# The low part of the keys in zero-filled tiles: a second scores pass over all 128 rows

## The chip, the cores and the metric

The kernel runs on one core of one Trainium2 chip. The metric is the time of one execution in device microseconds (us), taken as the median of several runs. One run was also recorded by the hardware profiler; its rows give start and length of each instruction on TensorE (PE, and PEld for its weight loads), VectorE (DVE), ScalarE (ACT) and GpSimd (POOL).

## The reference

Two blocks of two layers each work on 512 positions of width 1024. The parts that the change touches are the scores of three attentions:

```
# block 1: per head h of 6, head dim 64, three dilations mixed; per query row
scores = q_h @ k_h.T * 64**-0.5 - slope_h * distance          (masked)
# block 2, indexer: 8 heads of dim 64, one shared key
I[t, s] = sum_h w[t, h] * relu(q_idx[t, h] . k_idx[s])         (top 256 kept)
# block 2, sparse attention: 8 heads of dim 64
logits = q_h @ k_h.T * 64**-0.5                                (only the kept keys)
```

Around them lie dense projections (input, output, feed-forward), a depthwise convolution, a gated recurrence in each layer and normalisations. Inputs and outputs are float32.

## The kernel before

Activations are held channel-major: a tile is 128 channels (partitions) by 512 positions. TensorE takes float32 operands in a rounded form, so the kernel splits an operand into a high part H (the rounded value, cast on ScalarE) and a low part L (the remainder, a subtraction). A dense product is three matmuls per 128 channels, `mm3` at L332 to L334: H times H, L times H, H times L. Weights are loaded as `wraw`, split into `wH` (L311, ScalarE) and `wL` (L312, GpSimd), and used.

A head has 64 channels, so two heads (even and odd) share a 128-row tile, in rows 0 to 63 and 64 to 127. For the scores of one head, `q_part` builds a tile `qs` with the high part of its queries in the head's own 64 rows and the low part in the other 64 (L834, L835), and `qk_parts` builds `ks` with the high part of the keys in both halves (L845, L846). The first matmul of the scores (L894) takes all 128 rows: high queries times high keys plus low queries times high keys. The second (L895) adds high queries times low keys: it takes the 64 rows `r` of the head alone, since the low keys `kl` (L847) fill only those rows. The indexer does the same at L1291 and L1292, with low keys `kL` written into both halves once per layer (L1266).

The low keys are tiles of a rotating pool. In block 1 they share the tag `rS` with `qs`, `ks` and with the operands of the recurrence (L737, copied at L738), six buffers in all, one low tile for the two heads of a pair; in block 2 they have a tag `kl` of two buffers. `ltag` names it.

The order of the work comes from Python generators that are woven together with fixed costs: in block 1 the recurrence and then six heads of dilated attention (`heads(0)` for even and `heads(1)` for odd heads, the second two steps behind), the dense products that fill TensorE in between, and the convolution; in block 2 the indexer's eight heads beside dense products, and later eight heads of sparse attention beside dense products. After a head's scores come the softmax (`softmax_rows`: L856 on VectorE, L451 on ScalarE, L858 and L859 on VectorE), a transpose on TensorE (L867), a split of the weights (L311, L312) and the product with the values (L625, L626). Each engine executes its instructions in a fixed order, which the framework lays out when the kernel is built.

Of the kernel before, what the change touches and what calls it, by code (L numbers as in the profile page):

```python
# [9 lines left out]
F32 = mybir.dt.float32  # L10
F32R = mybir.dt.float32r
# [7 lines left out]
S = 512  # L19
# [228 lines left out]
class Net:  # L248
    def __init__(self, tc, I, out, es):
        self.tc, self.nc, self.I, self.out = tc, tc.nc, I, out  # L250
        self.n = 0
        self.other = self.pinned = self.unpin = None
        self.ntmp, self.vbufs, self.nv = 4, 2, 3
        self.qtag = self.ktag = self.ltag = ("rS", 6)
        self.pending = []
        self.gate = None
        nc = self.nc
        pool = lambda name, **k: es.enter_context(tc.tile_pool(name=name, bufs=1, **k))
        self.cp = pool("const")
        self.wp = pool("wts")  # L260
        self.hp = pool("hid")
        self.ps = pool("psum", space=PSUM)
        self.xd = es.enter_context(tc.tile_pool(name="xd", bufs=1, space=bass.MemoryType.DRAM))
        self.ident = self.one(self.cp, [128, 128], "ident")
        self.bones = self.one(self.cp, [128, 128], "bones")
        self.ones = self.one(self.cp, [128, 128], "ones")
        nc.vector.memset(self.ones, 1.0)
# [374 lines left out]
class Recurrence:  # L642
# [88 lines left out]
    def operands(self, n, Q, K):  # L731

        N, m = self.N, S // (2 * n)
        view = lambda t, d: pattern(t, 0, (d, 2), (2 * n, m), (1, n))
        out = []
        for t in (K, Q):
            x = N.tile(self.P, [128, S], "rS", 6)  # L737
            N.nc.scalar.copy(view(x, n), view(t, S + n))  # L738
            out.append(x)
        return out  # L740
# [95 lines left out]
    return qs, r  # L836


def qk_parts(N, P, q, k, kl, odd, scale):

    nc = N.nc
    qs, r = q_part(N, P, q, odd, scale)
    o = slice(0, 64) if odd else slice(64, 128)
    ks = N.tile(P, [128, S], *N.ktag, F32R)
    N.behind(nc.scalar.copy(ks[r], k[r]))  # L845
    N.behind(nc.scalar.copy(ks[o], k[r]))  # L846
    nc.vector.tensor_sub(kl[r], k[r], ks[r].bitcast(F32))  # L847
    return qs, ks, kl, r


def softmax_rows(N, P, p, bias, w):
# [17 lines left out]
    N.split(SH[:, :nk, o], SL[:, :nk, o], p[:, :nk])  # L869


def key_parts(N, P):
    return N.tile(P, [128, S], *N.ltag, F32R)


def attention_head(N, P, q, k, kl, vt, h, out, bias, e, causal):


    nc = N.nc
    v = head_values(N, P, vt, h)  # L880
    qh, kh, klo, r = qk_parts(N, P, q, k, kl, e == 1, 0.125)
    yield 1
    for a in range(2):
        W = weight_tiles(N, P)
        nk = 2 + 2 * a if causal else 4
        if causal:
            for y in W:
                nc.gpsimd.memset(y[:, nk - 1, :128].bitcast(F32), 0.0)
        for t in (2 * a, 2 * a + 1):
            tk = slice(128 * t, 128 * t + 128)  # L890
            n = t + 1 if causal else 4
            w, wm = 128 * n, max(256, 128 * n)
            p = N.bank("s")
            nc.tensor.matmul(p[:, :wm], qh[:, tk], kh[:, :wm], start=True, stop=False)  # L894
            nc.tensor.matmul(p[:, :wm], qh[r, tk], klo[r, :wm], start=False, stop=True)  # L895
            s = softmax_rows(N, P, p, bias(t), w)
            yield 1
            transpose_probs(N, s, n, t, *W)
            if t % 2:
                yield 1  # L900
                weighted_values(N, P, v, *W, out[:, 256 * a:256 * a + 256], nk)
        yield 1


def dilated_head(N, P, h, q, k, kl, vt, out):
    tab = N.tile(P, [128, 896], "rW", 2)
    N.nc.sync.dma_start(tab, N.I["alibi"][h])
    return attention_head(N, P, q, k, kl, vt, h + 6, out, lambda t: tab[:, 384 - 128 * t:896 - 128 * t], h % 2, False)


def opening(N, P, c, mod, vec):
# [34 lines left out]
def block1_layer(N, l, mod, vec, sib, src, step, hs, ready):  # L946
    nc, I = N.nc, N.I
    N.drop_x()
    with N.tc.tile_pool(name="mix1", bufs=1, reuse_waits="tile") as P:
# [3 lines left out]
            take(p)  # L953

        rec = Recurrence(N, P, vec, l, sib)
        vt, pads, qk = {}, [], {}
        orec = [N.tile(P, [128, S], "orec", 3) for _ in range(3)]
        oatt = [N.tile(P, [128, S], "oatt", 3) for _ in range(3)]
# [33 lines left out]
                yield from cm(base + j, take)  # L992
            qk[j] = ts

        sg, ys, kls, done = [], [None, None], {}, set()
        mixed, first = [], {}
        order = (5, 6, 7, 0, 1, 2, 3, 4)
        chain = itertools.chain
# [1 line left out]
        def heads(e):  # L1000
            if e == 0:
                for j in range(3):
                    yield from rec.pair(j, vt, orec[j])
                N.lnexp()
                done.add("rec")
            yield from ready_when(lambda: "rec" in done, 1)
            for j in range(3):
                yield from ready_when(lambda: j in qk and (2 * j + e + 6) // 4 in vt, 1)
                if j not in kls:
                    kls[j] = key_parts(N, P)  # L1010
                yield from dilated_head(N, P, 2 * j + e, *qk[j], kls[j], vt, oatt[j][64 * e:64 * e + 64])
                done.add((j, e))

        def conv():
# [228 lines left out]
def index_parts(N, P, p, rope):  # L1243

    nc = N.nc
    mc = N.tile(P, [128, S], "tmp", N.ntmp)
    nc.scalar.copy(mc, p)
    glr = N.tile(P, [96, 2, S], "W", 6, F32R)
    one = N.tile(P, [32, S], "tmp", N.ntmp)
    nc.gpsimd.memset(one, 1.0)  # L1250
    nc.vector.tensor_copy(one[:16], mc[96:112])
    stacked(N, glr[:, 0], one, (1, 0))
    p = N.bank("t", [128, 4, 32])
    for t in range(4):
        nc.tensor.transpose(p[:, t], mc[64:96, 128 * t:128 * t + 128], N.ident[64:96, 64:96])
    w8 = N.tile(P, [128, 4, 8], "w8", 1)
    nc.vector.tensor_scalar(w8, p[:, :, :8], 8.0 ** -0.5, None, op0=OP.mult)
    end = rope.begin(mc)
    kH = N.tile(P, [128, S], *N.ktag, F32R)
    kL = N.tile(P, [128, S], *N.ltag, F32R)  # L1260

    def keys():
        end()
        for r in (slice(0, 64), slice(64, 128)):
            nc.scalar.copy(kH[r], mc[:64])
            nc.vector.tensor_sub(kL[r], mc[:64], kH[:64].bitcast(F32))  # L1266
    return glr, w8, kH, kL, keys


def stacked(N, out, src, low):  # L1270
# [7 lines left out]
            nc.scalar.copy(o, src)  # L1278


def index_scores(N, P, iq, w8, kH, kL, sc):

    nc = N.nc
    for h in range(8):
        yield from ready_when(lambda: len(iq) > h // 2, 1)
        qs, r = q_part(N, P, iq[h // 2], h % 2, 0.125)
        for t in range(1, 4):
            w = 128 * (t + 1)
            tk = slice(128 * t, 128 * t + 128)
            p = N.bank("s")  # L1290
            nc.tensor.matmul(p[:, :w], qs[:, tk], kH[:, :w], start=True, stop=False)  # L1291
            nc.tensor.matmul(p[:, :w], qs[r, tk], kL[r, :w], start=False, stop=True)  # L1292
            y = N.tile(P, [128, S], "tmp", N.ntmp)
            nc.scalar.activation(y[:, :w], p[:, :w], AF.Relu)
            if h == 0:
                nc.vector.tensor_scalar(sc[t][:, :w], y[:, :w], w8[:, t, 0:1], None, op0=OP.mult)
            else:
                nc.vector.scalar_tensor_tensor(sc[t][:, :w], y[:, :w], w8[:, t, h:h + 1], sc[t][:, :w],
                                               op0=OP.mult, op1=OP.add)
            yield 1  # L1300
    for t in range(1, 4):
        w = 128 * (t + 1)
        nc.vector.memset(sc[t][:64, w - 64:w], -1e30)
# [16 lines left out]
def sparse_attention(N, P, aq, ak, vt, bias, outs):  # L1320
    def heads(e):
        for j in range(4):
            if j not in kl:
                kl[j] = key_parts(N, P)
                out[j] = N.tile(P, [128, S], "tmp", N.ntmp)
            yield from attention_head(N, P, aq[j], ak[j], kl[j], vt, 2 * j + e, out[j][64 * e:64 * e + 64],
                                      lambda t: bias[t][:, :128 * t + 128], e, True)
            done.add((j, e))
            if {(j, 0), (j, 1)} <= done:
                outs[j] = (N.tile(P, [128, S], "X", 8, F32R), N.tile(P, [128, S], "X", 8, F32R))  # L1330
                N.split(*outs[j], out[j], N.nc.gpsimd)

    kl, out, done = {}, {}, set()
    return heads(0), delay(heads(1), 5, 1)


# [208 lines left out]
def block2(N, hs, ready, out):  # L1545
    nc, I = N.nc, N.I
    N.ntmp, N.vbufs, N.nv = 4, 2, 4
    N.qtag, N.ktag, N.ltag = ("qs", 2), ("ks", 2), ("kl", 2)
    with N.tc.tile_pool(name="b2", bufs=1) as B:
        tri = N.one(B, [128, 128], "tri", F32R)  # L1550
        with N.tc.tile_pool(name="tri", bufs=1) as P:
# [12 lines left out]
        for l in range(2):  # L1564
# [5 lines left out]
            with N.tc.tile_pool(name="mix2", bufs=1, reuse_waits="tile") as P:  # L1570
# [4 lines left out]
                N.gate = None  # L1575
                sc = [b0] + [N.tile(P, [128, S], "sc", 3) for _ in range(3)]
                rope = Rope(N, P, tab)
                glr, *keys, parts = index_parts(N, P, ready[0], rope)
                N.soon(8, parts)
                gla = Gla(N, P, l, tri, chunks, vec)  # L1580
# [85 lines left out]
```

## Time and profile before

| | |
|---|---|
| median of 3 runs | 3408.36 us (3407.62 to 3408.36) |
| the profiled execution's own time | 3403.52 us |
| its span, first to last instruction | 3401.7 us |
| PE, DVE, POOL, ACT busy | 96%, 52%, 51%, 47% of the span |
| mean granted TensorE clock | 0.983 |

The busy time of TensorE is not to be read as TensorE at its peak: its rows are pipelined, so that two of them overlap, and their ends are modelled. What tells how long a matmul holds TensorE is the distance from its start to the start of the next one.

### The profile page before, as it was taken

To read this page: it belongs to the slowest core of one execution; us is meant where nothing else is said; L and a number is where in the kernel's file an instruction comes from. 1 tells how busy PE (TensorE), PEld (TensorE's weight loads), DVE (VectorE), ACT (ScalarE), POOL (GpSimd) and SP (SyncE) were. 2 spreads that over 40 slices of the span, in tenths; PEclk is the share of its full clock that TensorE was granted. 3 is DMA by queue.
4 is the path that set the end of the run, shared out by engine and by line. 5 is a ranking of instruction groups with operands and counts; after the bars stand their busy time and mean duration, and the time that the engine had idled before them with its cause. 6 is when DMAs were issued, how large, how long until landed. Compare 5 with 4: busy or idle time off the path is not lost.

```text
span 3401.7 us, 46240 instructions
## 1 busy us (share of the span) xinstructions
PE 3263.0 (96%) x16546; PEld 2655.2 (78%) x16546; DVE 1777.1 (52%) x3029; ACT 1589.6 (47%) x3104; POOL 1744.5 (51%) x1442
## 2 busy tenths in 40 slices
PE   8799999998899999999999999999999999999998
PEld 6677787787766888887878777888878787778887
DVE  8987677607976633226740735332367407353332
ACT  4457543334466544435343645443353436454433
POOL 5542366555542455553445447565634454476654
PEclk9899999999899999999999999999999999999999
DMA  6323355542212322332213132333322131322232
GB/s 231 108 71 99 115 176 178 179 132 97 87 46 68 103 99 96 99 108 86 87 57 101 52 108 81 98 97 93 102 76 87 57 101 51 108 81 98 96 94 80
DMA packets 174445, 338.92 MB, mean 100 GB/s; under 512 B 20388, under 2 KB 27428, under 8 KB 174215
## 3 DMA queue, kind: packets, MB, share of 16 engines
q1 hardware_dynamic: 174214, 335.97, 31.1%
q8 instruction: 130, 2.13, 0.3%
q14 instruction: 101, 0.82, 0.1%
HBM read 325.28 MB, written 8.91 MB: 98 GB/s over the span
## 4 chain that ended last, share of the span: by engine, by line
PE 76%; DVE 11%; issue 4%; ACT 3%; POOL 3%; DMA 2%; SPq 0%; POOLq 0%; ACTq 0%; DVEq 0%
PE p L332 22%; PE p L333 21%; PE p L334 21%; POOL wL L312 2%; DVE cv L566 2%; PE s L706 2%; DVE ada L528 1%; DMA ada<-in_w_ada 1%; PE s L1424 1%; PE s L895 1%; PE t L867 1%; PE o L625 1%; PE o L626 1%; PE s L894 1%; DVE rW L746 1%
## 5 line engine op out<-in xcount | busy, mean ns | idle before, releaser
L312 POOL TENSOR_TENSOR wL<-wraw,wH 128x512 fp32r<-128x512 f32 x996 | 1334.6, 1348 | 1278.4 <-ACT wH L311 1184.3
L332 PE MATMUL p<-hH,wH 128*128 128x512 f32 (+1 forms) x2808 | 1080.9, 386 | 12.2 <-ACT hH L311 7.5
L333 PE MATMUL p<-hL,wH 128*128 128x512 f32 (+1 forms) x2808 | 1069.5, 381 | 12.7 <-POOL hL L312 10.2
L334 PE MATMUL p<-hH,wL 128*128 128x512 f32 (+1 forms) x2808 | 1065.5, 380 | 6.2 <-POOL wL L312 6.2
L311 ACT CAST wH<-wraw 128x512 fp32r<-128x512 f32 x996 | 607.0, 613 | 947.9 <-PE p L333 436.9
L332 PEld LDWEIGHTS p<-hH,wH 128*128 128x128 f32 x2808 | 536.4, 191 | 122.4 <-issue 14.0
L333 PEld LDWEIGHTS p<-hL,wH 128*128 128x128 f32 x2808 | 537.4, 191 | 111.1 <-POOL hL L312 12.2
L334 PEld LDWEIGHTS p<-hH,wL 128*128 128x128 f32 x2808 | 536.8, 191 | 107.2 <-POOL wL L312 10.0
L1142 DVE SCALAR_TENSOR_TENSOR y<-p,vec,y 128x511 f32<-128x511 f32 (+1 forms) x264 | 196.8, 748 | 484.9 <-ACT y L1139 297.4
L332 PE MATMUL p<-aH,wH 128*128 128x512 f32 (+1 forms) x704 | 266.5, 379 | 2.9 <-ACT aH L311 2.9
L333 PE MATMUL p<-aL,wH 128*128 128x512 f32 (+1 forms) x704 | 266.5, 379 | 0.6 <-POOL aL L312 0.6
L334 PE MATMUL p<-aH,wL 128*128 128x512 f32 (+1 forms) x704 | 265.6, 377 | 0.6 <-POOL wL L312 0.6
L332 PE MATMUL p<-wH,hH 128*128 128x256 f32 x704 | 202.4, 287 | 0.0
L333 PE MATMUL p<-wL,hH 128*128 128x256 f32 x704 | 201.4, 286 | 0.0
L334 PE MATMUL p<-wH,hL 128*128 128x256 f32 x704 | 200.3, 284 | 0.0
L528 DVE SCALAR_TENSOR_TENSOR ada<-ada,c 128x1024 f32<-128x1024 f32 x96 | 144.2, 1502 | 44.3 <-DMA ada<-in_w_ada 43.6
L312 POOL TENSOR_TENSOR aL<-y,aH 128x512 fp32r<-128x512 f32 x88 | 113.9, 1295 | 98.2 <-ACT aH L311 98.2
L332 PEld LDWEIGHTS p<-aH,wH 128*128 128x128 f32 x704 | 133.2, 189 | 27.7 <-ACT aH L311 3.4
L333 PEld LDWEIGHTS p<-aL,wH 128*128 128x128 f32 x704 | 133.1, 189 | 25.8 <-POOL aL L312 1.1
L334 PEld LDWEIGHTS p<-aH,wL 128*128 128x128 f32 x704 | 133.1, 189 | 25.5 <-POOL wL L312 1.0
L706 PE MATMUL s<-rS,rS 64*128 64x128 f32 (+1 forms) x864 | 111.6, 317 | 33.9 <-DVE rW L761 21.2
L332 PEld LDWEIGHTS p<-wH,hH 128*128 128x128 f32 x704 | 135.8, 193 | 3.7 <-issue 2.9
(338 smaller groups left out, 4736.9 us busy)
## 6 DMA issues: line engine op xcount, KB each, us to landing
ada<-in_w_ada SPq DMA_DIRECT2D x96, 512.0 KB
wraw<-in_w1up SPq DMA_DIRECT2D x176, 256.0 KB
wraw<-in_w2up SPq DMA_DIRECT2D x176, 256.0 KB
wraw<-in_w2cm SPq DMA_DIRECT2D x164, 256.0 KB
wraw<-in_w1dn SPq DMA_DIRECT2D x80, 256.0 KB
wraw<-in_w2dn SPq DMA_DIRECT2D x80, 256.0 KB
wraw<-in_w1cm SPq DMA_DIRECT2D x72, 256.0 KB
wraw<-in_w2tm SPq DMA_DIRECT2D x64, 256.0 KB
```

The source lines that it names most:

```text
L311: self.nc.scalar.copy(H, src)
L312: (eng or self.nc.vector).tensor_sub(L, src, H.bitcast(F32))
L332: self.product = first = mm(out, a[0], b[0], start=start, stop=False, **kw)
L333: mm(out, a[0], b[1], start=False, stop=False, **kw)
L334: mm(out, a[1], b[0], start=False, stop=stop, **kw)
L528: ins = nc.vector.scalar_tensor_tensor(w, w, 1.0, c, op0=OP.mult, op1=OP.mult, accum_out=mod[:, j:j + 1])
L566: nc.vector.scalar_tensor_tensor(y, pad[:, j:j + S], w, y, op0=OP.mult, op1=OP.add)
L625: nc.tensor.matmul(o, v[:, i], SH[:, i], start=i == 0, stop=False)
L626: nc.tensor.matmul(o, v[:, i], SL[:, i], start=False, stop=i == n - 1)
L706: N.nc.tensor.matmul(p[:, at:at + w], K[r, ks], Q[r, qs], start=True, stop=True)
L746: nc.vector.tensor_mul(view(Q), view(Q), pattern(t, 1, (b - 1, 2), (2, m), (0, n)))
L1142: nc.vector.scalar_tensor_tensor(y[:, -d:], p[:, :S + d], c[:, i:i + 1], y[:, -d:], op0=OP.mult, op1=OP.add)
```

## The change

Two tiles `kz0` and `kz1` per layer replace the rotating low-key tiles. `low_keys` makes them at the start of a layer's mixing stage and fills with zeros, on GpSimd, the half that the heads of the other parity use: rows 64 to 127 of `kz0`, rows 0 to 63 of `kz1`. Even heads write their low keys into rows 0 to 63 of `kz0`, odd heads into rows 64 to 127 of `kz1`, so the other half stays zero. The second matmul of the scores then takes all 128 rows of `qs` and of `kz`; the low queries meet zeros. The tag `rS` gets five buffers in place of six, the tag `kl` goes away. Nothing else is edited.

```diff
-        self.qtag = self.ktag = self.ltag = ("rS", 6)
+        self.qtag = self.ktag = ("rS", 5)
...
-            x = N.tile(self.P, [128, S], "rS", 6)
+            x = N.tile(self.P, [128, S], "rS", 5)
...
+def low_keys(N, P):
+    N.kz = [N.one(P, [128, S], f"kz{e}", F32R) for e in range(2)]
+    for e, t in enumerate(N.kz):
+        N.nc.gpsimd.memset(t[64 - 64 * e:128 - 64 * e].bitcast(F32), 0.0)
...
+    kl = N.kz[odd]
     nc.vector.tensor_sub(kl[r], k[r], ks[r].bitcast(F32))
-    return qs, ks, kl, r
+    return qs, ks, kl
...
-            nc.tensor.matmul(p[:, :wm], qh[r, tk], klo[r, :wm], start=False, stop=True)
+            nc.tensor.matmul(p[:, :wm], qh[:, tk], kl[:, :wm], start=False, stop=True)
...
         rec = Recurrence(N, P, vec, l, sib)
+        low_keys(N, P)
...
-        for r in (slice(0, 64), slice(64, 128)):
+        for kl, r in zip(N.kz, (slice(0, 64), slice(64, 128))):
             nc.scalar.copy(kH[r], mc[:64])
-            nc.vector.tensor_sub(kL[r], mc[:64], kH[:64].bitcast(F32))
+            nc.vector.tensor_sub(kl[r], mc[:64], kH[:64].bitcast(F32))
...
-            nc.tensor.matmul(p[:, :w], qs[r, tk], kL[r, :w], start=False, stop=True)
+            nc.tensor.matmul(p[:, :w], qs[:, tk], N.kz[h % 2][:, :w], start=False, stop=True)
...
-    N.qtag, N.ktag, N.ltag = ("qs", 2), ("ks", 2), ("kl", 2)
+    N.qtag, N.ktag = ("qs", 2), ("ks", 2)
...
                 rope = Rope(N, P, tab)
+                low_keys(N, P)
```

## Rows read from the trace of the kernel before

**Rows 1.** The page: the span, and each engine's busy time.

```profile
span 3401.7 us, 46240 instructions
PE 3263.0 (96%) x16546; PEld 2655.2 (78%) x16546; DVE 1777.1 (52%) x3029; ACT 1589.6 (47%) x3104; POOL 1744.5 (51%) x1442
```

**Rows 2.** Windows: stretch, length, busy PE, PEld, DVE, ACT, POOL, clock, DMA.

```profile
274.00:352.00 78.00, 73.51 (x354) 51.06 (x353) 65.25 (x156) 58.33 (x125) 17.25 (x16) 1.00 0.27 85
1030.00:1116.00 86.00, 82.18 (x403) 59.05 (x402) 60.17 (x142) 59.27 (x128) 19.62 (x17) 0.98 0.20 62
1540.00:1610.00 70.00, 67.80 (x307) 47.81 (x306) 46.39 (x68) 44.61 (x84) 23.88 (x21) 1.00 0.21 62
1868.00:1960.00 92.00, 91.42 (x429) 65.67 (x428) 65.42 (x188) 61.47 (x153) 36.58 (x54) 1.00 0.17 55
```

**Rows 3.** Waits of PE, 274 to 352 us: total, times, longest.

```profile
PE t L867 <- DVE W L312: 1.6, 3, 0.9
PE s L894 <- ACT rS L846: 1.5, 2, 0.8
```

**Rows 4.** Lines L895 and L1292 by themselves: count, shortest/median/longest ns, shapes.

```profile
L895 PE MATMUL s<-kl,qs x64: 379/410/502, 1871.7 to 2892.7; 64*128 64x256 f32 x32, 64*128 64x384 f32 x16, 64*128 64x512 f32 x16
L895 PE MATMUL s<-rS,rS x48: 490/496/502, 276.3 to 1113.4; 64*128 64x512 f32 x48
L1292 PE MATMUL s<-kl,qs x48: 379/438/502, 1557.7 to 2544.4; 64*128 64x256 f32 x16, 64*128 64x384 f32 x16, 64*128 64x512 f32 x16
```

**Rows 5.** Timeline of PE, dilated attention, layer 0: start, length, instruction.

```profile
282.60 0.39 PE L332 MATMUL p<-hH,wH 128*128 128x512 f32 x1
282.83 0.39 PE L333 MATMUL p<-hL,wH 128*128 128x512 f32 x1
...
284.42 0.39 PE L894 MATMUL s<-rS,rS 128*128 128x512 f32 x1
284.74 0.49 PE L895 MATMUL s<-rS,rS 64*128 64x512 f32 x1
285.16 0.50 PE L332 MATMUL p<-hH,wH 128*128 128x512 f32 x1
285.50 0.40 PE L333 MATMUL p<-hL,wH 128*128 128x512 f32 x1
```

**Rows 6.** The same stretch, weight loads (PEld).

```profile
282.83 0.19 PEld L334 LDWEIGHTS p<-hH,wL 128*128 128x128 f32 x1
...
284.74 0.18 PEld L895 LDWEIGHTS s<-rS,rS 64*128 64x128 f32 x1 [0.36 <-issue]
285.16 0.19 PEld L332 LDWEIGHTS p<-hH,wH 128*128 128x128 f32 x1 [0.24 <-issue]
```

**Rows 7.** Timeline of PE: 256 columns, dense, then sparse attention.

```profile
69.61 0.28 PE L332 MATMUL p<-wH,hH 128*128 128x256 f32 x1
69.73 0.28 PE L333 MATMUL p<-wL,hH 128*128 128x256 f32 x1
...
1883.86 0.28 PE L894 MATMUL s<-ks,qs 128*128 128x256 f32 x1
1884.07 0.38 PE L895 MATMUL s<-kl,qs 64*128 64x256 f32 x1
1884.38 0.50 PE L332 MATMUL p<-G,wH 128*128 128x512 f32 x1
1884.72 0.39 PE L333 MATMUL p<-G,wH 128*128 128x512 f32 x1
```

**Rows 8.** Timeline of POOL, start of block 2's first layer.

```profile
1540.24 1.46 POOL L1211 MEMSET swap<- 128x512 f32 x3
...
1544.14 1.30 POOL L312 TENSOR_TENSOR wL<-wraw,wH 128x512 fp32r<-128x512 f32 x1 [1.51 <-ACT wH L311]
```

**Rows 9.** Waits in the recurrence of layer 0, 100 to 274 us.

```profile
POOL rK L747 <- ACT rS L738: 34.2, 13, 10.0
ACT rS L738 <- PE s L706: 26.5, 11, 12.6
PE s L706 <- DVE rW L761: 12.5, 8, 6.9
```

More of the change, by code (lines that the diff above doesn't have):

```diff
@@ L836, in q_part, with qk_parts @@
     return qs, r
-def qk_parts(N, P, q, k, kl, odd, scale):
+def low_keys(N, P):
+    N.kz = [N.one(P, [128, S], f"kz{e}", F32R) for e in range(2)]
+    for e, t in enumerate(N.kz):
+        N.nc.gpsimd.memset(t[64 - 64 * e:128 - 64 * e].bitcast(F32), 0.0)
+def qk_parts(N, P, q, k, odd, scale):
     nc = N.nc
@@ L869, in transpose_probs, with attention_head @@
     N.split(SH[:, :nk, o], SL[:, :nk, o], p[:, :nk])
-def key_parts(N, P):
-    return N.tile(P, [128, S], *N.ltag, F32R)
-def attention_head(N, P, q, k, kl, vt, h, out, bias, e, causal):
+def attention_head(N, P, q, k, vt, h, out, bias, e, causal):
     nc = N.nc
     v = head_values(N, P, vt, h)
-    qh, kh, klo, r = qk_parts(N, P, q, k, kl, e == 1, 0.125)
+    qh, kh, kl = qk_parts(N, P, q, k, e == 1, 0.125)
     yield 1
@@ L902, in attention_head, with dilated_head @@
         yield 1
-def dilated_head(N, P, h, q, k, kl, vt, out):
+def dilated_head(N, P, h, q, k, vt, out):
     tab = N.tile(P, [128, 896], "rW", 2)
     N.nc.sync.dma_start(tab, N.I["alibi"][h])
-    return attention_head(N, P, q, k, kl, vt, h + 6, out, lambda t: tab[:, 384 - 128 * t:896 - 128 * t], h % 2, False)
+    return attention_head(N, P, q, k, vt, h + 6, out, lambda t: tab[:, 384 - 128 * t:896 - 128 * t], h % 2, False)
 def opening(N, P, c, mod, vec):
@@ L993, in qk_in @@
             qk[j] = ts
-        sg, ys, kls, done = [], [None, None], {}, set()
+        sg, ys, done = [], [None, None], set()
         mixed, first = [], {}
@@ L1008, in heads @@
                 yield from ready_when(lambda: j in qk and (2 * j + e + 6) // 4 in vt, 1)
-                if j not in kls:
-                    kls[j] = key_parts(N, P)
-                yield from dilated_head(N, P, 2 * j + e, *qk[j], kls[j], vt, oatt[j][64 * e:64 * e + 64])
+                yield from dilated_head(N, P, 2 * j + e, *qk[j], vt, oatt[j][64 * e:64 * e + 64])
                 done.add((j, e))
@@ L1259, in index_parts @@
     kH = N.tile(P, [128, S], *N.ktag, F32R)
-    kL = N.tile(P, [128, S], *N.ltag, F32R)
     def keys():
         end()
-        for r in (slice(0, 64), slice(64, 128)):
+        for kl, r in zip(N.kz, (slice(0, 64), slice(64, 128))):
             nc.scalar.copy(kH[r], mc[:64])
-            nc.vector.tensor_sub(kL[r], mc[:64], kH[:64].bitcast(F32))
-    return glr, w8, kH, kL, keys
+            nc.vector.tensor_sub(kl[r], mc[:64], kH[:64].bitcast(F32))
+    return glr, w8, kH, keys
 def stacked(N, out, src, low):
@@ L1278, in stacked, with index_scores @@
             nc.scalar.copy(o, src)
-def index_scores(N, P, iq, w8, kH, kL, sc):
+def index_scores(N, P, iq, w8, kH, sc):
     nc = N.nc
@@ L1285, in index_scores @@
         yield from ready_when(lambda: len(iq) > h // 2, 1)
-        qs, r = q_part(N, P, iq[h // 2], h % 2, 0.125)
+        qs, _ = q_part(N, P, iq[h // 2], h % 2, 0.125)
         for t in range(1, 4):
@@ L1322, in heads @@
         for j in range(4):
-            if j not in kl:
-                kl[j] = key_parts(N, P)
+            if j not in out:
                 out[j] = N.tile(P, [128, S], "tmp", N.ntmp)
-            yield from attention_head(N, P, aq[j], ak[j], kl[j], vt, 2 * j + e, out[j][64 * e:64 * e + 64],
+            yield from attention_head(N, P, aq[j], ak[j], vt, 2 * j + e, out[j][64 * e:64 * e + 64],
                                       lambda t: bias[t][:, :128 * t + 128], e, True)
@@ L1331, in heads @@
                 N.split(*outs[j], out[j], N.nc.gpsimd)
-    kl, out, done = {}, {}, set()
+    out, done = {}, set()
     return heads(0), delay(heads(1), 5, 1)
```

## The prediction

> **What bounds the kernel now.** I read the page first. It shows TensorE busy for 96% of the span and every other engine for about half of it [rows 1], so TensorE's queue sets the time unless a stage says otherwise. The windows over the stages that the change touches come next: dilated attention in two layers of block 1, the indexer and sparse attention in two layers of block 2 (the second layer of block 2 repeats the first). In each the reader is to compare the PE column with the length of the stretch: 73.51 of 78 us, 82.18 of 86, 67.80 of 70, 91.42 of 92, with the clock at 0.98 or 1.00 [rows 2]. VectorE is the next engine: 65.25 of 78 us at its highest, and 46 to 65 us elsewhere. The waits of TensorE itself are short: in the first stretch the two largest come to 1.6 and 1.5 us in all [rows 3]. So a microsecond taken out of TensorE's queue in these stages is nearly a microsecond off the end, except where the next instruction stood waiting for VectorE or ScalarE already.
>
> **What a 64-row pass costs now.** The second pass runs 160 times: 48 in dilated attention, 48 in the indexer, 64 in sparse attention [rows 4]. Its length in the row, about 0.5 us at 512 columns, isn't its cost; the distances between starts are. Two dense matmuls of 512 columns follow each other in 0.23 us. Around the 64-row pass the distances are 0.32 us from L894 to L895, 0.42 from L895 to the dense L332, 0.34 from that to L333 [rows 5]. The three together take 1.08 us where three full passes at 0.23 would take 0.69: 0.39 us too much. The weight loads tell why: in the dense stream the load for the next matmul starts with the one that runs (282.83 in both lists), while the load of L895 comes 0.36 us late and that of the L332 behind it 0.24 us late, with no engine named as the cause [rows 6]. TensorE doesn't put a load under a running matmul where the next matmul changes from 128 rows to 64 or back. At 256 columns the excess is the same: 0.21, 0.31 and 0.34 us against 0.12, 0.12 and 0.23, again 0.39 [rows 7]. So it doesn't depend on the width and I use 0.39 for all 160.
>
> **What the change does to TensorE.** The pass keeps its columns and takes 128 rows, as the first pass and the dense matmuls do. It isn't in the trace, so I bound it: at best it follows and is followed at the dense distance, which gives back 0.39 us; at worst its load stays exposed on both sides as now and nothing comes back. Its nearest row is the dense L333 behind L332: the same shape, the same element type, both with loads of 0.19 us that hide [rows 5, 6]. I take 0.39. The sum is 48 x 0.39 = 18.7 us for dilated attention, 18.7 for the indexer, 64 x 0.39 = 25.0 for sparse attention: 62.4 us of TensorE's queue.
>
> A rule speaks against the last step. The Trainium skill ("TensorE: Matmul & The Clock Gate", Part 3, The mechanism) says that a weight load overlaps a running matmul only if the two use different row groups. By it the full-height load before each second pass would be exposed, 0.19 us each, and the one behind it too. The dense rows, in which a 128-row load starts together with a 128-row matmul, do not bear it out, and the sum goes by the rows.
>
> **What of it is absorbed.** Where TensorE already waits for another engine, a shorter queue only lengthens the wait. In dilated attention about a third of the pairs (16 of 48) lie at the ends of the stages, where the filling products thin out and where TensorE's waits of rows 3 stand; I take half of their 6.2 us as lost, 3 us. VectorE in layer 0 would be busy for 65.25 of 68.6 us, and its queue will hold up some softmaxes: 2 us more. In the indexer the waits at its start might grow by half a microsecond a layer: 1 us. In sparse attention TensorE is busy for 91.42 of 92 us, VectorE would be at 65.4 of 79.5 [rows 2], and I take nothing off. That leaves 18.7 - 5 = 13.7, 18.7 - 1 = 17.7 and 25.0: 56.4 us.
>
> **The other edits.** The eight memsets of 64x512 (two in each of four layers) are new on POOL. The nearest row is the memset of a full 128x512 tile, three in 1.46 us; half the rows may cost as much, so I take 0 to 0.5 us each. At the start of block 2 they stand ahead of the split of `wL`, which now waits 1.51 us for ScalarE [rows 8]: two memsets fit in that, and I cost them at nothing. If that cover were gone, they would add 4 us at most. The memsets also wait until the memory under `kz` is free. Whatever lay there belongs to the stage before, and its last readers are the normalisation and the matmuls that must end before this stage's dense products start. The subtraction L847 into `kz` must wait for the last L895 of the previous head of that parity; VectorE has by then done that head's softmax, which waited for the same matmul, so nothing is added. The fifth buffer of `rS`: in block 1 the attention no longer takes a low tile from it, so four tiles per pair of heads go through five buffers where five went through six. In the recurrence, which takes two per level, the second copy of a level must now wait for the products of two levels before instead of three. ScalarE waits there for L706 already, 26.5 us in layer 0, and POOL waits behind it [rows 9]. But TensorE's own wait is for VectorE's L761, and a copy that starts when the products of two levels before end is early for its own. I cost it at nothing here and keep it as a rival.
>
> **The sum.** 3403.52 us of the profiled execution less 56.4 is 3347; that execution was 4.8 us under the median of the runs, so against 3408.36 I predict 3352 us.
>
> **The rivals.**
> *Absorbed by half.* VectorE and ScalarE become the bound where they are near it: the softmax chain between the scores and the transpose doesn't get shorter. For it speaks VectorE's 84% in the first stretch; against it, that TensorE's waits for these engines are a few us per stage. Half of 56 us leaves 3380. Part of this case is that the framework lays the engines' order out anew, and some of it falls worse.
> *No gain from the load.* A full-height pass with the same stationary data can't have its load under the pass before, 0.19 us exposed ahead of it and 0.19 behind, which is 0.38 of the 0.39 us: 160 x 0.19 = 30 us back and 3382 if one of the two, about 3408 if both. The dense rows speak against it: `wH` is loaded for L332 and again for L333, and both hide. The skill's rule named above is this one.
> *Slower, by the recurrence.* Five buffers make ScalarE's copies wait for products one level later, ScalarE's queue stands, and what stands behind it (weight casts, POOL's L747) starves TensorE. There are 54 operand pairs in two layers (three pairs of heads, nine each). To be slower than 3415 the loss must reach 56 + 7 = 63 us, 1.2 us of TensorE's time per operand pair. The 12.6 us that one such wait lasted [rows 9] shows that it could be; that TensorE's wait there is for VectorE speaks against.
>
> **How the numbers follow.** The full saving, less or more what is absorbed (3338 to 3366), has 0.68; absorbed by half or more (3366 to 3401), 0.24, of which 0.02 is the exposed load; no change, 0.03; slower, 0.05. What can be told from no change is about 0.2%, 6.8 us. The lower end 3338 is all 62.4 us and 8 more from shorter waits or a luckier order. The upper end 3384 takes in the case of one half. Faster 0.92, same 0.03, slower 0.05.
>
> **What would show it.** In the changed profile the distance from the first to the second pass should be 0.23 us at 512 columns and 0.12 at 256, the two behind it 0.23, and the late loads at these lines gone. The stretches of rows 2 should be shorter by about 7, 8, 9 and 12 us, and VectorE's share higher in each. POOL's memsets should end before the next `wL` is due. The prediction is wrong if the second pass still stands 0.3 us behind the first, if TensorE's waits for L312, L846 or L835 grow by more than 10 us, or if the recurrence of block 1, which holds no scores, gets longer by more than a few us.

## The result and the profile after

The changed kernel takes 3363.8 us, median of four runs (3361.02 to 3365.97), against 3407.99 (3403.18 to 3408.36) for the kernel before beside it: a ratio of 0.9873, 95% interval 0.9856 to 0.989, 44 us faster. The prediction was 3352 us with a range of 3338 to 3384. The page of the changed kernel, its span and busy times, beside [rows 1]:

```profile
span 3361.2 us, 46241 instructions
PE 3209.5 (95%) x16546; PEld 2649.6 (79%) x16546; DVE 1764.1 (52%) x3029; ACT 1586.2 (47%) x3105; POOL 1748.0 (52%) x1450
```

The counts of TensorE are the same; only its busy time falls, and POOL has eight more instructions, the memsets (ACT has one more). The lines have moved: L894 and L895 are now L898 and L899, L1292 is L1294, the transpose L867 is L875, the softmax L856, L858, L859 is L864, L866, L867, and the low keys' L847 is L855.

The second passes by themselves (count, shortest/median/longest ns, shapes), beside [rows 4]:

```profile
L899 PE MATMUL s<-kz,qs x64: 276/336/423, 1851.5 to 2854.7; 128*128 128x256 f32 x32, 128*128 128x384 f32 x16, 128*128 128x512 f32 x16
L899 PE MATMUL s<-kz,rS x48: 388/393/629, 274.8 to 1098.4; 128*128 128x512 f32 x48
L1294 PE MATMUL s<-kz,qs x48: 275/337/397, 1544.6 to 2512.0; 128*128 128x256 f32 x16, 128*128 128x384 f32 x16, 128*128 128x512 f32 x16
```

TensorE's timeline in sparse attention, with a 256-column and a 512-column pair, beside [rows 5, 7]:

```profile
1859.58 0.39 PE L334 MATMUL p<-G,wL 128*128 128x512 f32 x1
1859.81 0.28 PE L898 MATMUL s<-ks,qs 128*128 128x256 f32 x1
1859.92 0.28 PE L899 MATMUL s<-kz,qs 128*128 128x256 f32 x1
1860.04 0.39 PE L332 MATMUL p<-G,wH 128*128 128x512 f32 x1
1860.27 0.39 PE L333 MATMUL p<-G,wH 128*128 128x512 f32 x1
1860.50 0.40 PE L334 MATMUL p<-G,wL 128*128 128x512 f32 x1
1860.74 0.39 PE L898 MATMUL s<-ks,qs 128*128 128x512 f32 x1
1860.97 0.40 PE L899 MATMUL s<-kz,qs 128*128 128x512 f32 x1
```

The weight loads of the same stretch, beside [rows 6]:

```profile
1859.81 0.19 PEld L899 LDWEIGHTS s<-kz,qs 128*128 128x128 f32 x1
1859.93 0.19 PEld L332 LDWEIGHTS p<-G,wH 128*128 128x128 f32 x1
1860.04 0.19 PEld L333 LDWEIGHTS p<-G,wH 128*128 128x128 f32 x1
```

From the first pass to the second it is now 0.23 us at 512 columns (1860.74 to 1860.97) and 0.11 at 256; the next dense matmul follows the 256-column pass in 0.12, the one behind it in 0.23. The load of L899 starts with the first pass (1859.81 in both lists), that of L332 with L899. Over all 160 pairs the median distance from first to second pass fell from 0.33, 0.27 and 0.21 us (512, 384, 256 columns) to 0.23, 0.18 and 0.12.

The windows of the four stages, with the columns of [rows 2]; they hold about the same work as there, by the count of TensorE's rows, and are shorter by 4, 4, 7 and 5 us:

```profile
272.00:346.00 74.00, 68.35 (x361) 53.48 (x360) 65.46 (x154) 57.94 (x126) 17.29 (x16) 0.98 0.27 90
1018.00:1100.00 82.00, 76.08 (x407) 60.39 (x406) 57.85 (x137) 58.81 (x126) 21.26 (x18) 0.96 0.19 62
1527.00:1590.00 63.00, 59.70 (x302) 46.96 (x301) 45.19 (x67) 43.85 (x84) 24.33 (x22) 1.00 0.22 66
1847.00:1934.00 87.00, 82.89 (x432) 64.33 (x431) 64.92 (x188) 61.43 (x153) 36.05 (x54) 1.00 0.18 58
```

TensorE's idle share has grown: 4.1 us of 87 in the last stretch, where [rows 2] left 0.58 of 92. The question is for whom it waits. The scores of sparse attention in layer 0, first to last, before and after; the same 401 rows of TensorE:

```profile
1871.50:1957.00 85.50, 84.92 (x401) 60.82 (x399) 62.75 (x179) 57.53 (x144) 34.28 (x52) 1.00 0.16 52
1851.40:1931.50 80.10, 75.99 (x401) 58.89 (x399) 62.45 (x179) 57.08 (x144) 34.00 (x52) 1.00 0.16 53
```

TensorE's waits in the second of them (total, times, longest):

```profile
PE t L875 <- DVE W L312: 2.2, 4, 1.0
PE s L898 <- DVE st L864: 0.6, 2, 0.5
PE t L875 <- DVE st L866: 0.6, 2, 0.5
PE o L625 <- ACT W L311: 0.2, 1, 0.2
PE t L875 <- DVE tmp L867: 0.2, 1, 0.2
```

In the kernel before, the same work (1871.5 to 1957 us) has one such row:

```profile
PE t L867 <- DVE W L312: 0.4, 2, 0.2
```

The chain that ended last, followed back from the kernel's end, says the same more strongly. Its shares of these two stretches by line, first before, then after (each list goes on beyond its last entry here):

```profile
by line: PE p L332 19.3%; PE p L333 16.4%; PE p L334 16.0%; PE s L895 11.9%; PE t L867 9.8%; PE o L625 6.1%; PE s L894 6.0%; PE o L626 5.2%; DVE kl L847 2.6%; DVE tmp L859 1.8%; DVE W L312 1.3%; DVE st L1606 0.8%; issue 0.7%; ACT W L311 0.6
```

```profile
by line: DVE tmp L867 11.5%; PE p L334 9.3%; PE p L333 8.8%; PE p L332 8.2%; DVE tmp L864 7.9%; PE t L875 6.7%; PE o L625 6.5%; PE o L626 5.4%; DVE W L312 5.3%; DVE kz L855 5.2%; issue 3.6%; DVE qs L835 3.1%; PE s L898 2.8%; ACT tmp L451 2.
```

Before, the listed lines of TensorE make 90.7% of the stretch; after, they make 47.7% and VectorE's 33.0%, with the softmax's scaling L867 first. The chain went over to the softmax within a stage in which VectorE is busy for 62 of 80 us.

The stages by time, in us, worked out from TensorE's timeline of each run ("e1" and so on are the experiments below, by their first letters; e6 and e10 are edits of the kernel before). The recurrence runs from its first product to the first scores, dilated attention from there to the first product of the next normalisation, the indexer from its first scores to the first product of the linear attention, that one to the first sparse scores, and "sparse+out" from there to the next normalisation; "scores alone" ends with the first pass of the last pair, so that 31 of a layer's 32 second passes lie in it:

```
                 before  e1     e10    e6     after  e5     e7     e8     e9     e11    e12
recurrence 0     194.7  197.0  196.1  195.1  192.8  196.1  194.8  196.9  195.2  196.9  194.8
dilated 0        120.8  124.6  125.0  125.0  117.1  116.9  117.6  113.9  117.6  117.1  117.5
recurrence 1     217.9  213.1  213.5  217.7  214.1  213.1  213.4  206.5  213.9  213.7  213.4
dilated 1        122.5  123.1  124.8  124.0  118.9  119.4  117.9  117.0  118.4  118.7  118.9
indexer 0        123.0  123.0  123.0  123.0  116.0  115.9  115.9  119.8  115.9  115.9  115.9
linear att. 0    191.1  191.1  191.1  191.1  191.1  191.1  178.6  191.1  191.1  179.3  179.3
sparse+out 0     201.5  201.2  201.5  200.1  195.5  191.3  196.2  194.6  204.4  194.2  194.1
  scores alone    85.4   85.5   85.4   82.7   80.0   74.0   80.0   77.4   87.2   82.4   79.9
indexer 1        123.1  123.0  123.1  123.0  115.9  115.9  115.9  120.0  115.9  115.8  115.9
linear att. 1    191.1  191.1  191.1  191.1  191.1  191.1  178.6  191.1  191.1  179.3  179.3
sparse+out 1     202.1  202.1  201.8  200.0  194.4  190.9  196.2  194.6  205.1  193.8  193.7
  scores alone    85.5   85.6   85.6   82.7   80.1   74.0   80.2   77.4   87.7   82.1   79.3
```

After less before: dilated -3.7 and -3.6, recurrence -1.9 and -3.8, indexer -7.0 and -7.2, sparse -6.0 and -7.7; together 40.9 of the 40.5 us between the spans. In block 2 the indexer, the linear attention and the scores repeat to some tenths where nothing of theirs is edited, "sparse+out" to 2 us (194.4 and 196.2 in layer 1 for after and e7). Dilated attention of layer 0 differs by some 4 us between runs of the same code (120.8 and 125.0 for before and e6), so a single pair of profiles says less there.

That difference goes with TensorE's clock. The whole stage in layer 0, of before, e10 (64 rows as well) and after; the clock is the third number from the end:

```profile
276.00:396.70 120.70, 112.53 (x557) 83.68 (x556) 87.58 (x192) 76.16 (x158) 37.88 (x31) 0.99 0.37 120
278.10:403.10 125.00, 115.52 (x557) 86.24 (x556) 87.51 (x192) 76.19 (x158) 37.80 (x31) 0.96 0.35 116
274.60:391.70 117.10, 107.52 (x557) 86.22 (x556) 88.09 (x192) 75.33 (x158) 37.85 (x31) 0.96 0.38 124
```

A mean of 0.96 says that part of the stretch ran at the lower of two levels, 1.2 in place of 2.4 GHz. The six profiles with a 64-row pass there (before, e4, e10, e1, e6, e3) were granted 0.99, 0.97, 0.96, 0.95, 0.95 and 0.93 and took 120.8, 122.7, 125.0, 124.6, 125.0 and 126.2 us. At 0.96, 125.0 became 117.1: 7.9 us.

### The profile page after: what moved, and what is told of

The parts are those of the page before. It is cut to its first block, busy times and chain, and to the rows that moved or that the text cites. A ratio compares the mean times of both kernels' runs of the same rounds, so it can differ in the third digit from the quotient of the medians.

```text
span 3361.2 us, 46241 instructions
## 1 busy us (share of the span) xinstructions
PE 3209.5 (95%) x16546; PEld 2649.6 (79%) x16546; DVE 1764.1 (52%) x3029; ACT 1586.2 (47%) x3105; POOL 1748.0 (52%) x1450
## 4 chain that ended last, share of the span: by engine, by line
PE 73%; DVE 16%; ACT 4%; DMA 3%; issue 3%; POOL 2%; SPq 0%; ACTq 0%; POOLq 0%; DVEq 0%
PE p L332 21%; PE p L333 21%; PE p L334 21%; DVE ada L528 2%; DVE cv L566 2%; PE s L706 2%; DMA ada<-in_w_ada 2%; PE s L1425 1%; POOL wL L312 1%; DVE W L312 1%; PE o L625 1%; DVE tmp L867 1%; PE t L875 1%; PE o L626 1%; DVE x L1534 1%
## 5 line engine op out<-in xcount | busy, mean ns | idle before, releaser
L312 POOL TENSOR_TENSOR wL<-wraw,wH 128x512 fp32r<-128x512 f32 x996 | 1333.3, 1347 | 1229.8 <-ACT wH L311 1120.5
L332 PE MATMUL p<-hH,wH 128*128 128x512 f32 (+1 forms) x2808 | 1074.4, 384 | 14.4 <-ACT hH L311 9.7
L333 PE MATMUL p<-hL,wH 128*128 128x512 f32 (+1 forms) x2808 | 1068.6, 381 | 10.6 <-POOL hL L312 7.8
L332 PEld LDWEIGHTS p<-hH,wH 128*128 128x128 f32 x2808 | 535.9, 191 | 115.0 <-ACT hH L311 12.4
L332 PE MATMUL p<-aH,wH 128*128 128x512 f32 (+1 forms) x704 | 266.0, 378 | 3.3 <-ACT aH L311 3.3
L332 PE MATMUL p<-wH,hH 128*128 128x256 f32 x704 | 200.7, 285 | 0.0
L312 POOL TENSOR_TENSOR aL<-y,aH 128x512 fp32r<-128x512 f32 x88 | 113.8, 1293 | 98.3 <-ACT aH L311 98.3
L332 PEld LDWEIGHTS p<-aH,wH 128*128 128x128 f32 x704 | 132.8, 189 | 27.8 <-ACT aH L311 3.8
L706 PEld LDWEIGHTS s<-rS,rS 64*128 64x128 f32 x864 | 86.5, 200 | 66.0 <-DVE rW L761 22.7
```

The lines of the kernel that those rows point to most:

```text
L312: (eng or self.nc.vector).tensor_sub(L, src, H.bitcast(F32))
L332: self.product = first = mm(out, a[0], b[0], start=start, stop=False, **kw)
L333: mm(out, a[0], b[1], start=False, stop=False, **kw)
L706: N.nc.tensor.matmul(p[:, at:at + w], K[r, ks], Q[r, qs], start=True, stop=True)
```

## The experiments

Theory A: each full pass gives back 0.39 us of TensorE's queue, and part of it is lost to the softmax chain between the scores and the transpose. Rival B: the zero-filled tiles and the new order cost the part that is missing. Rival C: each stage by itself gives back everything.

**e1_tiles_only.** The changed kernel with both second passes back on 64 rows:

```diff
-            nc.tensor.matmul(p[:, :wm], qh[:, tk], kl[:, :wm], start=False, stop=True)
+            r = slice(64 * e, 64 * e + 64)
+            nc.tensor.matmul(p[:, :wm], qh[r, tk], kl[r, :wm], start=False, stop=True)
...
-            nc.tensor.matmul(p[:, :w], qs[:, tk], N.kz[h % 2][:, :w], start=False, stop=True)
+            r = slice(64 * (h % 2), 64 * (h % 2) + 64)
+            nc.tensor.matmul(p[:, :w], qs[r, tk], N.kz[h % 2][r, :w], start=False, stop=True)
```

> The new tiles, memsets and five buffers, but both second passes on 64 rows as before. Theory A (the full-height pass gives 0.39 us of TensorE's queue each, the waits for the softmax take part of it back, and the tiles are worth only what the recurrence gained): 3396 to 3406 us, the recurrence of block 1 shorter by 2 and 4 us, every other stage within 1 us of before. Rival B (the new tiles and the order laid out for them cost what is missing of the 62 us): 3413 to 3430 us.

It took 3405.87 us against 3406.84: 0.9999 (0.999 to 1.0009). The tiles, memsets and five buffers together are worth nothing that can be measured, and B falls. Recurrence 1 is shorter by 4.8 us, about as A had expected. Recurrence 0 is longer by 2.3 and dilated 0 by 3.8 (at a granted clock of 0.95 against 0.99), which it hadn't; the stages of block 2 did not move.

**e3_index_only and e4_sparse_only.** e3 takes back the attention's half of that edit alone, so that only the indexer's pass is full. e4 leaves only sparse attention's full:

```diff
+            r = slice(0, 128) if causal else slice(64 * e, 64 * e + 64)
+            nc.tensor.matmul(p[:, :wm], qh[r, tk], kl[r, :wm], start=False, stop=True)
```

> Full-height second pass in the indexer alone; the attentions stay on 64 rows. Theory A: the run with the tiles alone less 12 to 15 us, all of it between the first and the last indexer matmul of each layer (6 to 7 us each). Rival C (queue time comes back in full when the stage stands by itself, and is lost only where stages follow each other): less 18 to 19 us.

> Full-height second pass in sparse attention alone. Theory A: the run with the tiles alone less 10 to 15 us, with TensorE's waits for L312 and the softmax in these two stages up by 4 to 6 us each, as in the changed kernel. Rival C: less 23 to 25 us and no new waits.

e3: 3393.16 us, 0.9965 (0.9953 to 0.9977), 12.7 us under e1; the indexer takes 115.9 us in both layers, 7.1 less, as in the changed kernel. e4: 3391.46, 0.996 (0.9945 to 0.9974), 14.4 under e1; its two sparse stages are shorter by 5.0 and 5.6 us, the scores by 5.6, with the same waits as after (L875 for L312 2.2 us, L898 for L864 0.6; 3.8 in all, 3.4 more than before, where A had expected 4 to 6). C falls: 18.7 and 25.0 don't come back even when each stands alone. So the loss arises within each stage.

**e5_after_no_scaling and e6_before_no_scaling.** In both kernels the reciprocal and the scaling of the softmax are left out in sparse attention, so its weights aren't normalised; one link of the chain is gone and VectorE has less to do:

```diff
-    nc.vector.reciprocal(st[:, 2:3], st[:, 1:2])
-    nc.vector.tensor_scalar(s, s, st[:, 2:3], None, op0=OP.mult)
+    if scale:
+        nc.vector.reciprocal(st[:, 2:3], st[:, 1:2])
+        nc.vector.tensor_scalar(s, s, st[:, 2:3], None, op0=OP.mult)
```

> The changed kernel without the division by the sum in the softmax of sparse attention (64 reciprocals and 64 scalings on VectorE are left out, so these outputs are not scaled). Theory A: the chain from scores to transpose is shorter by 0.7 us, the new waits shrink, each sparse stage gets 3 to 6 us shorter than in the changed kernel, about 3354 us in all. Rival B: within 2 us of the changed kernel, 3362 to 3366, since the order and the tiles are what costs.

> The kernel before without the division by the sum in the softmax of sparse attention (same work left out as in the changed kernel's run without it). Theory A (TensorE's queue was the bound of sparse attention before the change, the softmax chain is after it): each sparse stage within 2 us of before, 3403 to 3408 us. Rival (VectorE held these stages up already): 4 to 6 us less per stage, as it was on the changed kernel, 3396 us.

On the changed kernel (3360.42 us, one run) the scores go from 80.0 to 74.0 us in both layers, on the kernel before (3401.16, one run) from 85.4 to 82.7. Not all of that is the scaling. In e5 and e6 alike the order is laid out anew: eight dense passes of 512 columns stand outside the stretch and two more transposes in it, about 1.6 us of work by the distances between starts. That leaves 4.4 us in the changed kernel and 1.1 in the kernel before. (The whole of "sparse+out", where the work is the same, is shorter by 4.2 and 3.5 us in e5, as A had expected, and by 1.4 and 2.1 in e6. As a whole e5 was to take about 3354 us; it has 3.3 us more than after in recurrence 0.) Within each pair the work is the same: without the scaling the full pass returns 82.7 - 74.0 = 8.7 us of the 12.1 of 31 passes, with it 5.4. In e5, TensorE's waits in that stretch are nearly gone, and the chain is TensorE's again (lines from the softmax on are numbered one higher there):

```profile
PE t L876 <- ACT tmp L451: 0.6, 2, 0.4
PE t L876 <- DVE W L312: 0.2, 1, 0.2
```

```profile
by line: PE p L334 16.1%; PE p L332 15.6%; PE p L333 15.5%; PE t L876 10.2%; PE o L625 7.4%; PE o L626 6.0%; PE s L900 5.4%; PE s L899 5.3%; ACT tmp L451 3.4%; ACT W L311 3.0%; issue 2.7%; ACT ks L852 1.7%; ACT lo L628 1.5%; DVE tmp L864 1.
```

That the kernel before also gains 1.1 us of waits and late starts, where TensorE's waits came to 0.4, shows that a little of the softmax stood in its way already.

**e9_scaling_on_gpsimd.** Whether it is VectorE's load or the chain's length: the scaling of sparse attention moves from VectorE to GpSimd.

```diff
-    nc.vector.tensor_scalar(s, s, st[:, 2:3], None, op0=OP.mult)
+    (nc.gpsimd if pool else nc.vector).tensor_scalar(s, s, st[:, 2:3], None, op0=OP.mult)
```

> The changed kernel with the scaling of the softmax of sparse attention on GpSimd: VectorE has 64 instructions of about 0.5 us less, but the chain from the scores to the transpose gets longer by about 0.8 us. If VectorE's queue is what absorbs the gain, each sparse stage gets 2 to 5 us shorter, about 3357 us. If the length of the chain is, each gets 1 to 4 us longer, 3366 to 3372 us.

3380.82 us, 0.9923 (0.9904 to 0.9942), 17 us worse than the changed kernel. The scores take 87.2 and 87.7 us, 7.2 and 7.6 more, though here too 1.6 us of work stand outside; "sparse+out" is longer by 8.9 and 10.7, where 1 to 4 had been expected. VectorE's busy time falls from 62.45 to 50.19 us in that stretch, and TensorE waits the longer:

```profile
1853.40:1940.70 87.30, 75.27 (x395) 57.45 (x393) 50.19 (x151) 58.40 (x146) 65.39 (x81) 1.00 0.15 49
```

```profile
PE t L875 <- POOL tmp L867: 10.5, 11, 1.8
```

The scaling takes 1170 ns on GpSimd (mean of 30 in this stretch) against 571 on VectorE (29 in the same work of the changed kernel). A longer link costs, though VectorE is relieved: the length of the chain counts. That VectorE's load has no share beside it isn't shown, since no run relieves VectorE at the same length.

**e8_two_transpose_banks.** All transposes go through one bank, which is free again when L312 has read it; here they get two, and the dense products three in place of four:

```diff
-OPEN_TAGS = "ppppssto"
+OPEN_TAGS = "pppsstto"
...
-BANKS = {"p": 4, "s": 2, "t": 1, "o": 1}
+BANKS = {"p": 3, "s": 2, "t": 2, "o": 1}
```

> The changed kernel with two banks for the transposes and three instead of four for the dense products. If the new wait in sparse attention is for the single bank that a transpose writes (freed by VectorE's subtraction L312): the waits of the transposes for L312 go, and each sparse stage is 2 to 4 us shorter than in the changed kernel. Rival (VectorE's queue is what is late, whatever the bank): less than 1 us. Dense stages may lose by the bank; read by stage.

The scores go from 80.0 to 77.4 us in both layers, and the transposes' wait for L312 is gone; in its place TensorE waits 1.2 us for L312 ahead of the values and 1.2 for L867. Of the 2.6 us, 1.6 are work that stands outside the stretch, as in e5; "sparse+out" changes by -0.9 and +0.2, where 2 to 4 less had been expected. The kernel as a whole is slower than the changed one (3371.8 us; 0.9899, 0.9882 to 0.9916): the indexer takes 3.8 and 4.1 us more, and what follows the last sparse stage 4.2. So the one bank holds about 1 us of the missing part in a layer, and a bank for the dense products is worth more.

**e10_before_five_buffers.** The kernel before with the tag `rS` at five buffers and its low keys in a tag of their own:

```diff
-        self.qtag = self.ktag = self.ltag = ("rS", 6)
+        self.qtag = self.ktag = ("rS", 5)
+        self.ltag = ("kl", 2)
...
-            x = N.tile(self.P, [128, S], "rS", 6)
+            x = N.tile(self.P, [128, S], "rS", 5)
```

> The kernel before with five buffers of rS in place of six and a pool of two for the low keys (64 rows, not zero-filled, 64-row second pass). If the shorter recurrence of layer 1 and the longer first layer of the run with the tiles alone come from the buffers and the order laid out for them, not from the zero-filled tiles: recurrence of layer 1 near 213 us instead of 218, recurrence and dilated attention of layer 0 together some 4 to 6 us longer than before, about 3406 us in all. If they come from the zero-filled tiles: all stages within 1 us of before.

3404.47 us beside 3405.92 (one run). Recurrence 1 takes 213.5 us, 4.4 less than before, as in every kernel with five buffers (212.9 to 214.1, e8 aside) and in none with six (217.9, 217.7). So that shift comes with the buffers, not with the zeros or the full pass. Recurrence 0 and dilated 0 went the other way by 5.6 together, most of it in dilated 0, at the clock of 0.96 shown above.

**e7_gla_full_height.** The same form elsewhere: the state products of the linear attention of block 2 (64 of them in a layer, in 32 pairs) take 64 rows. A second set of key tiles holds the other chunk's rows with zeros:

```diff
+                self.kz = [self.N.tile(self.P, [128, S], "G", 16) for _ in range(4)]
+                for z in self.kz:
+                    self.N.nc.gpsimd.memset(z[:64], 0.0)
...
-                self.N.nc.vector.tensor_mul(o, o, ps[t])
+                self.N.nc.vector.tensor_mul(z[64:, c], o[64:, c], ps[t][64:])
+                self.N.nc.vector.tensor_mul(o[:64, c], o[:64, c], ps[t][:64])
+                self.N.nc.gpsimd.memset(o[64:, c], 0.0)
...
-                mm(p, self.kd[t][r, 128 * h:128 * h + 128], self.vt[h][r, t], start=True, stop=True)
+                mm(p, (self.kd, self.kz)[c % 2][t][:, 128 * h:128 * h + 128], self.vt[h][:, t], start=True, stop=True)
```

> The changed kernel with the gated linear attention's state products on 128 rows too: a second set of key tiles with zeros in the rows of the other chunk, 64 products per run that change from 128 rows to 64 and back now. There TensorE is busy for all of the stage and VectorE for a third, so Theory A gives the whole queue time back: 64 x 0.3 to 0.4 us, 19 to 25 us off the changed kernel, 3339 to 3345 us. Rival (only the fp32r passes lose time at the change of rows, a float32 product hides it; or a stage gives back two thirds at most): 0 to 12 us off.

3341.61 us, 0.9811 (0.9796 to 0.9827), 22 us under the changed kernel. The stage takes 178.6 us in place of 191.1: 12.5 = 32 x 0.39, all of it, in both layers (the whole kernel is shorter by 22 of these 25 us). TensorE's timeline, first of the kernel before, then of this one:

```profile
1686.98 0.40 PE L334 MATMUL p<-hH,wL 128*128 128x512 f32 x1
1687.31 0.70 PE L1424 MATMUL s<-V,G 64*128 64x256 f32 x2
1687.93 0.66 PE L1449 MATMUL o<-G,st 128*128 128x64 f32 x4
1688.40 0.48 PE L332 MATMUL p<-hH,wH 128*128 128x512 f32 x1
```

```profile
1677.33 0.40 PE L334 MATMUL p<-hH,wL 128*128 128x512 f32 x1
1677.57 0.59 PE L1432 MATMUL s<-V,G 128*128 128x256 f32 x2
1678.00 0.55 PE L1457 MATMUL t<-G,st 128*128 128x64 f32 x4
1678.36 0.47 PE L332 MATMUL p<-hH,wH 128*128 128x512 f32 x1
```

The distances 0.33, 0.62, 0.47 become 0.24, 0.43, 0.36: 0.39 us for a pair of passes. In this stage TensorE is busy for all of a stretch and waits for nobody, and VectorE is busy for less than half (window of this kernel):

```profile
1670.00:1730.00 60.00, 60.00 (x326) 52.05 (x326) 28.18 (x53) 25.85 (x65) 20.71 (x18) 1.00 0.20 60
```

**e11_heads_spread_34 and e12_heads_spread_less.** On top of e7 the fixed costs by which sparse attention's heads are woven in are made smaller, so that a head's steps stand further apart: 30 and 32 in e11 (its label names another size), 34 and 36 in e12, in place of 38 and 40.

```diff
-MIX2 = (40, 16, 8, 40, 38, 40, 96)
+MIX2 = (40, 16, 8, 40, 34, 36, 96)
```

> The kernel with the full-height state products, and the weave of sparse attention with fewer head steps per dense step (costs 30 and 32 instead of 38 and 40). More dense work then lies between a head's scores and its transposes. If the length of the softmax chain against the distance between the steps is what absorbs the gain: the stage from the first sparse score to the next normalisation gets 4 to 6 us shorter in each layer (from 196 to about 191), about 3331 us in all. If VectorE's or ScalarE's throughput or the order absorbs it: within 2 us, 3340 to 3344.

> The same with costs 34 and 36: by the same theory 2 to 4 us off each of the two stages, 3334 to 3338; by the other 3340 to 3344.

e11: 3334.65 us, 0.9795 (0.978 to 0.9809). e12: 3333.09, 0.9793 (0.9776 to 0.981), the lowest median of all. The sparse stages ("sparse+out") are shorter by 2.0 and 2.4 us in e11, where 4 to 6 had been expected, and by 2.1 and 2.5 in e12, where it was 2 to 4. The scores alone can't be compared with e7's, since more dense products lie among them; TensorE's idle time in them fell from 4.1 and 4.3 us to 2.8 and 2.6 in e11, 3.5 and 3.1 in e12. Distance gives back some of what the chain took, less than hoped. As whole kernels e7, e11 and e12 have intervals that overlap.

## Why the prediction was right, point by point

**The price of a pass: right.** The distances are those foretold, both loads hide, and the 0.39 us leave TensorE's queue at every pair, to come back in full where nothing stands in the way (e7). The exposed load didn't come: the 128-row load of L899 starts together with the 128-row matmul ahead of it and costs nothing. The rule of the Trainium skill ("TensorE: Matmul & The Clock Gate", Part 3, The mechanism), that a load overlaps a running matmul only if their row groups differ, is not borne out here, as in the dense rows; the same section names a background weight buffer as another way to load ahead, and no run here tells whether these loads go that way. Two slips changed nothing. The 0.36 and 0.24 us that the prediction calls lateness are idle times of the load unit; by their starts the two loads come 0.32 and 0.42 us behind the matmul under which they would hide. And 30 us back from 3408 would be 3378, not 3382.

**Sparse attention: the step that was mis-sized.** "I take nothing off" gave 25.0 us. The stages returned 6.0 + 7.7 = 13.7, and 10.6 when they changed alone (e4). The argument was that TensorE is busy for 91.42 of 92 us and VectorE would be at 65.4 of 79.5. But a share of TensorE near one says that the others are in time now, not how late they are once its own work in the scores is 12.1 us of 85 shorter. Between a tile's scores and its transpose stand L864, L451, L866 and L867 in turn, then L312 before the one transpose bank is free; the order lays a fixed amount of TensorE's work beside them. When that work shrinks, the chain doesn't. TensorE's waits rose from 0.4 to 3.8 us in layer 0, half of the 12.1 - 5.4 = 6.7 us missing from its scores, and the chain of waits passed to VectorE's lines.

The other half doesn't show as idle time, but the starts show it. Take for each pass the distance of rows that follow without a wait (0.2325, 0.175 and 0.1175 us for 512, 384 and 256 columns, 0.108 for a transpose): the stretch holds 71.1 us of such work in both kernels. What lies on top was 14.3 us before, 12.1 of it at the 64-row passes and 2.2 elsewhere; after, it is 8.9, all elsewhere. The growth by 6.7 us is the missing part, about half of it ahead of transposes. TensorE's idle time grew by 3.5 of it, from 0.6 to 4.1. The rest hides, because a row is drawn longer than its distance (0.39 against 0.23 us at 512 columns): a start late by up to 0.16 us leaves no gap.

The scaling accounts for 8.7 - 5.4 = 3.3 of the 6.7 us, together with the other order of e5 and e6, and the second bank for about 1 (each tried alone; they needn't add up). This is the rival "absorbed by half", in one stage.

**The indexer: right, a little high.** 17.7 foretold, 14.2 measured, the same in every kernel with its pass full, e8 aside. TensorE's waits grew there from 2.2 to 3.1 us (0.5 a layer foretold, 0.9 measured in layer 0). Counted by starts as above, what lies on top elsewhere grew from 3.1 to 5.6 us, so that the 2.3 us missing in a layer are again late starts, most of them without a gap; who delays them no run isolated.

**Dilated attention: about right, but not to be read from two profiles.** 13.7 foretold, 7.3 from before to after. Of six kernels with a 64-row pass there (before, e1, e3, e4, e6, e10; e3 has 126.2 and 124.7, e4 122.7 and 122.8) the means are 124.1 and 123.7 us, of six with a full one and the same banks (after, e5, e7, e9, e11, e12) 117.3 and 118.7: 6.8 + 5.0 = 11.8. The profiled execution of before was at the low end in layer 0, with the highest clock of its group. The clock is also a cost that the prediction has no term for. In layer 1 the granted clock of the stage is 0.99 in all six of the first group and 0.97 in all six of the second (0.99 in e8), which takes at most some 2 us of 119 (an estimate, 0.02 x 119). It fell once among the scores of either kernel, behind a thin stretch: TensorE was busy for 3.67 of 7 us before (1083.2 to 1090.2) and for 3.82 after (1068.9 to 1075.9), where it stayed low for longer. TensorE's waits at the stage of [rows 3] grew in one place, by 1.2 us (272 to 346 us):

```profile
PE t L875 <- DVE W L312: 2.8, 5, 1.1
PE s L898 <- ACT rS L853: 1.5, 2, 0.8
```

**The other edits: nothing, in sum.** e1 shows it to some 3.4 us (0.1% either way). The memsets stand ahead of the split of `wL`, as said, and fit into its wait: it starts 3.96 us behind the memset of `swap`, where it was 3.90 (POOL's timeline at the start of block 2, to be read beside [rows 8]):

```profile
1526.50 1.46 POOL L1214 MEMSET swap<- 128x512 f32 x3
1528.02 1.09 POOL L843 MEMSET kz<- 64x512 f32 x2
...
1530.46 1.29 POOL L312 TENSOR_TENSOR wL<-wraw,wH 128x512 fp32r<-128x512 f32 x1 [0.42 <-POOL tmp L1350]
```

The fifth buffer was costed at nothing and given to a rival as a loss. In layer 0 the single longest wait of each kind in [rows 9] did grow, and TensorE's in sum from 12.5 to 18.6 us:

```profile
POOL rK L747 <- ACT rS L738: 39.7, 16, 11.6
ACT rS L738 <- PE s L706: 25.1, 9, 17.2
PE s L706 <- DVE rW L761: 18.6, 7, 13.4
```

Yet the recurrence of layer 0 was longer by 2.3 us at most in any run with five buffers, and that of layer 1 was shorter by 3.8 us or more in all of them. Why five buffers make it so stays open: the whole order of block 1 is laid out anew with them.

**The sum.** By the profiles of before and after, 56.4 foretold and 40.9 measured differ by -6.4 (dilated), +5.7 (recurrence), -3.5 (indexer) and -11.3 (sparse). Were the dilated term read from the means, sparse attention would be the only large miss. The time lies in the range because its upper end took in the case of one half; that the recurrence, put at nothing, was shorter by 5.7 us made up for half of the sparse miss, and that was luck.

## What to carry to other kernels

A lone pass over 64 rows among 128-row matmuls costs three late starts; where its operand can be filled up with zeros, make it full, and look for the same form in every other stage: here the linear attention gave 25 us more in its two stages, the full sum, and 22 in the kernel's time, since nothing but TensorE set the time of those stages. To see how much of a shorter queue will reach the end, don't go by busy shares alone: follow one tile through the other engines' operations, compare that length with the TensorE work laid beside it, and look at whether the chain of waits of that stage already holds lines of another engine. What the chain absorbs is given back by shortening it or by setting its steps further apart, and only in part. And before the lengths of a stretch in two kernels are compared, count the rows in it and read the granted clock: 1.6 us of the gains in e5, e6 and e8 were work moved elsewhere, and some 4 us between two runs of dilated attention went with the clock.

## What the runs showed of the hardware

A 96-row pass shows none of the 64-row pass's excess. In the changed kernel's timeline of TensorE, at the indexer, it follows in 0.23 us and is followed in 0.24:

```profile
1552.72 0.39 PE L332 MATMUL p<-hH,wH 128*128 128x512 f32 x1
1552.95 0.40 PE L1357 MATMUL o<-W 96*128 96x512 f32 x1
1553.19 0.40 PE L333 MATMUL p<-hL,wH 128*128 128x512 f32 x1
```

The excess of 0.39 us was the same at 256, 384 and 512 columns, and for the state products of e7, where two 64-row passes of 256 columns stand together. A product of two float32 tiles that are not rounded, as the state products are, holds TensorE about twice as long: at 128 rows the second of a pair in e7 starts 0.215 us behind the first (median of 64, 256 columns), against 0.12 for the rounded form. And a memset of half the rows took POOL as long as one of all of them: two of 64x512 in 1.09 us, three of 128x512 in 1.46.
